# Retention and RWKV-7 mixer: a shorter chain from the keys to the decayed products, and head outputs summed in one PSUM bank

## The chip, the cores and the metric

The kernel runs on one core of a Trainium2 chip. The core has five engines with their own instruction queues: TensorE (matmuls, PE in the profile, with PEld for its weight loads), VectorE (DVE), ScalarE (ACT), GpSimd (POOL) and SyncE (SP), which only issues DMAs here. Matmul results go to PSUM, which has eight banks; everything else works in SBUF. The metric is the device time of one execution in microseconds (us); smaller is better.

## The reference

The program computes a decoder trunk of two layers for 1024 tokens of width 1024, in float32. Layer 0 is a mixer of two head groups that share one input projection: eight retention heads and eight RWKV-7 heads of 64 dimensions. Layer 1 is sliding-window attention. A SwiGLU network follows each. Only the mixer of layer 0 is changed. Of it, these are the lines that matter:

```python
decay = jnp.exp(-jnp.exp(w_log))
a = jax.nn.sigmoid(a0 + al @ a_up)
kkf = heads(kr * k_k)
kk = kkf / jnp.maximum(jnp.linalg.norm(kkf, axis=-1, keepdims=True), 1e-12)
kr = kr * (1.0 + (a - 1.0) * k_a)
# per token: state = state * w + (state @ a_t) b_t + v k, with a_t = -kk, b_t = kk * a
y = rwkv7_scan(r_h, heads(decay), k_h, v_h, -kk, kk * heads(a))
o = o_inner + o_cross          # retention: inside a chunk, and from the state before it
```

The decay of a token is exp(-c s), with c = exp(-0.5) and s the sigmoid of a projected value. Inside a chunk of 64 tokens the kernel needs the products of decays up to and including each token (the inclusive ones) and up to the token before it (the exclusive ones), and the reciprocals of the inclusive ones.

## The kernel before, in words

Channels lie on the 128 partitions and tokens in the free dimension. The sequence is worked in two halves of 512 tokens. A pair is two heads, one on partitions 0 to 63 and one on 64 to 127; there are four pairs of RWKV heads and four of retention heads for each half, so eight of each in all. A pair's tile is 128x512: eight chunks of 64 tokens for RWKV, four of 128 for retention.

`mixer0` sets up generators and lets the `Plan` class order them. Jobs are input projections (line 239 is the helper through which all mixer matmuls go; a job is 24 matmuls of 128x512 into a bank of the PSUM tag "f"). Chains are generators that yield after each step the events they need and a delay. The planner keeps an estimated time, advanced by each matmul. It runs the next step of a chain when its events and delay have passed and `room()` says that fewer than three PSUM tiles of the tag "m" were opened in the last 3 us of that estimate, and otherwise three matmuls of the current job. After the program is traced, the compiler's scheduler fixes each engine's order and gives out the tiles' memory: a tag has so many buffers, and a new tile of it has to wait until one is released. Each engine then works in its fixed order.

- `pair` (from line 655) is the chain of one RWKV pair. Step 1 (lines 666 to 676): scales the keys by the column kk, squares them (line 668), takes two tanh, turns one into the sigmoid s (673), scans it to its running sum in each chunk (cs, line 675), and subtracts s from that on GpSimd (676), which gives the running sum without the own token. Step 2 (680 to 702): sums of squares over a head by a matmul with a block matrix, their reciprocal root by Ln and Exp (682, 683), three exponentials (inclusive decays pw 685, their reciprocals 686, exclusive decays 687), the last inclusive decay of each chunk (PC, 689), the normalized keys (690), the products AR (692) and BK (693 to 696, copied by 697, other keys 701 and 702). Step 3 multiplies AR with BK on TensorE. Step 4 (729) multiplies r with pw on GpSimd into AR's other half. Later steps build masked products GG (754), their transposes and the values UV.
- `unit` (from line 813) takes two pairs of one half: it inverts triangular blocks on VectorE (836, 840), runs the recurrence over the eight chunks (938), and then forms the head outputs y (945 to 959): a sum within the chunk, from UV and GG, and one from the state before it, from GT and AR. Each sum has a PSUM bank; ScalarE copies one out (955), VectorE adds the other (956), ScalarE squares the result (958). Normalization and gate follow.
- `ret` is the chain of one retention pair; lines 1088 to 1099 form its outputs in the same way, with ScalarE's copy at 1096, VectorE's addition at 1097 and the square at 1099.

In these chains the short-lived 128x512 tiles have the tag "rt" with six buffers: kk, rn, s, ta, cs and pw of a pair, and y and q of a unit's two pairs. GpSimd also splits weights for the projections (331), after a cast on ScalarE (330).

## Time and profile before

| | us |
|---|---|
| median of three timed runs | 2411.41 |
| the three runs | 2411.33, 2411.41, 2417.50 |
| the profiled execution | 2407.97 |
| its span, first to last instruction | 2406.2 |

| engine | busy in the span, us | share |
|---|---|---|
| TensorE matmul | 2327.4 | 97% |
| TensorE weight loads | 1836.9 | 76% |
| VectorE | 1631.0 | 68% |
| ScalarE | 1036.0 | 43% |
| GpSimd | 1208.5 | 50% |

A row of a group of instructions in the profile reads: line, engine, operation, output tile <- input tiles, count, then least, median and greatest duration in ns, first and last start in us, and shape. A row of the timeline reads: start, duration, engine, line, operation, tiles, shape and count of like instructions in a row, and in brackets the idle time before it and what ended that. A row of waits reads: the waiting engine with its output tile and line, what it waited for, then the total in us, the number of waits and the longest. Busy time of TensorE has modelled ends, so a busy TensorE isn't one at its peak. The granted clock of TensorE is a share of full speed; its mean over the span is 0.988.

### The profile page before, as it was taken

To read this page: it belongs to the slowest core of one execution; us is meant where nothing else is said; L and a number is where in the kernel's file an instruction comes from. 1 tells how busy PE (TensorE), PEld (TensorE's weight loads), DVE (VectorE), ACT (ScalarE), POOL (GpSimd) and SP (SyncE) were. 2 spreads that over 40 slices of the span, in tenths; PEclk is the share of its full clock that TensorE was granted. 3 is DMA by queue.
4 is the path that set the end of the run, shared out by engine and by line. 5 is a ranking of instruction groups with operands and counts; after the bars stand their busy time and mean duration, and the time that the engine had idled before them with its cause. 6 is when DMAs were issued, how large, how long until landed. Compare 5 with 4: busy or idle time off the path is not lost. (4 is left out here: it accounts for less than half of the span.)

```text
span 2406.2 us, 35718 instructions
## 1 busy us (share of the span) xinstructions
PE 2327.4 (97%) x13098; PEld 1836.9 (76%) x13098; DVE 1631.0 (68%) x2478; ACT 1036.0 (43%) x1914; POOL 1208.5 (50%) x975
## 2 busy tenths in 40 slices
PE   8899999989999999999999999999999999999997
PEld 6676767777777888888778877677688788887785
DVE  5766765766557457887675459558628788888666
ACT  5353543223555433333333545456635233333336
POOL 6555332221443047776577632342231677777666
PEclk9999999999999999999999999999999999999999
DMA  7564543444345645553564322132236466646652
GB/s 250 197 214 171 165 155 123 143 119 124 122 171 166 213 155 207 215 204 135 198 249 148 127 75 64 53 134 67 94 123 216 158 215 217 215 182 248 242 201 108
DMA packets 167742, 395.93 MB, mean 165 GB/s; under 512 B 42896, under 2 KB 45584, under 8 KB 167568
## 3 DMA queue, kind: packets, MB, share of 16 engines
q1 hardware_dynamic: 164448, 388.15, 47.5%
q10 hardware_dynamic: 2832, 4.45, 0.5%
q8 instruction: 104, 1.70, 0.3%
q0 software_dynamic: 288, 1.05, 0.1%
q14 instruction: 70, 0.57, 0.1%
HBM read 271.29 MB, written 116.92 MB: 161 GB/s over the span
## 5 line engine op out<-in xcount | busy, mean ns | idle before, releaser
L331 POOL TENSOR_TENSOR w<-wr,w 128x512 fp32r<-128x512 f32 x196 | 266.3, 1365 | 444.3 <-ACT w L330 386.7
L239 PE MATMUL ps_f<-n,w 128*128 128x512 f32 x1440 | 384.4, 415 | 13.6 <-ACT w L330 5.9
L239 PEld LDWEIGHTS ps_f<-n,w 128*128 128x128 f32 x1440 | 268.4, 192 | 97.1 <-issue 22.0
L330 ACT CAST w<-wr 128x512 fp32r<-128x512 f32 x244 | 147.9, 612 | 180.1 <-PE ps_f L347 74.1
L331 POOL TENSOR_TENSOR w<-wq,w 128x512 fp32r<-128x512 f32 x92 | 130.0, 1424 | 32.6 <-ACT w L330 28.1
L345 PE MATMUL ps_f<-n,w 128*128 128x512 f32 x356 | 141.6, 398 | 2.4 <-ACT n L351 1.5
L346 PE MATMUL ps_f<-n,w 128*128 128x512 f32 x356 | 142.0, 399 | 0.0
L347 PE MATMUL ps_f<-n,w 128*128 128x512 f32 x356 | 140.5, 395 | 0.0
L1169 PE MATMUL ps_f<-n,w 128*128 128x512 f32 x322 | 127.1, 396 | 4.5 <-DVE h L1369 2.2
L1176 DVE TENSOR_TENSOR nq<-ps_m,u 128x512 f32<-128x512 f32 x88 | 58.8, 684 | 105.8 <-PE ps_m L1171 105.7
L1170 PE MATMUL ps_f<-n,w 128*128 128x512 f32 x322 | 126.3, 392 | 0.0
L1171 PE MATMUL ps_f<-n,w 128*128 128x512 f32 x322 | 125.6, 391 | 0.0
L353 POOL TENSOR_TENSOR n<-nq,n 128x512 fp32r<-128x512 f32 x64 | 107.0, 1684 | 10.7 <-ACT n L351 10.7
L1169 PE MATMUL ps_m<-n,w 128*128 128x512 f32 x282 | 110.5, 392 | 0.0
L1171 PE MATMUL ps_m<-n,w 128*128 128x512 f32 x282 | 109.9, 390 | 0.0
L1170 PE MATMUL ps_m<-n,w 128*128 128x512 f32 x282 | 109.7, 389 | 0.0
L331 POOL TENSOR_TENSOR wx<-wr,wx 128x512 fp32r<-128x512 f32 (+1 forms) x38 | 49.3, 1298 | 104.4 <-ACT wx L330 97.7
L1169 PE MATMUL ps_m<-cb,w 128*128 128x512 f32 x240 | 93.5, 389 | 0.9 <-DVE nq L1176 0.9
L1170 PE MATMUL ps_m<-cb,w 128*128 128x512 f32 x240 | 93.4, 389 | 0.0
L1171 PE MATMUL ps_m<-cb,w 128*128 128x512 f32 x240 | 93.4, 389 | 0.0
L1343 POOL TENSOR_TENSOR w<-wd,w 128x512 fp32r<-128x512 f32 (+1 forms) x53 | 76.5, 1455 | 33.3 <-ACT w L1342 33.3
L345 PEld LDWEIGHTS ps_f<-n,w 128*128 128x128 f32 x356 | 67.1, 189 | 20.1 <-issue 2.2
(525 smaller groups left out, 6496.8 us busy)
## 6 DMA issues: line engine op xcount, KB each, us to landing
hc<-n SPq DMA_DIRECT2D x74, 512.0 KB, 2.6
wsp<-w SPq DMA_DIRECT2D x54, 512.0 KB, 3.4
w<-wsp SPq DMA_DIRECT2D x54, 512.0 KB, 3.8
wq<-in_w_gate SPq DMA_DIRECT2D x44, 512.0 KB, 4.3
u<-u SPq DMA_DIRECT2D x88, 256.0 KB, 3.0
n<-hc SPq DMA_DIRECT2D x43, 512.0 KB, 5.4
wr<-in_w_in SPq DMA_DIRECT2D x34, 512.0 KB, 4.6
hid<-n SPq DMA_DIRECT2D x66, 256.0 KB, 2.0
```

Of the source, the lines that this page charges most:

```text
L239: self.nc.tensor.matmul(out, lhsT, rhs, **kw)
L330: nc.scalar.copy(hi[:, :n], raw[:, c])
L331: self.lo.tensor_tensor(out=lo[:, :n], in0=raw[:, c], in1=hi.bitcast(F32)[:, :n], op=ALU.subtract)
L345: nc.tensor.matmul(ps, hi, rh, start=k == 0, stop=False)
L346: nc.tensor.matmul(ps, hi, rl, start=False, stop=False)
L347: nc.tensor.matmul(ps, lo, rh, start=False, stop=k == n - 1)
L353: e.tensor_tensor(out=lo, in0=src, in1=hi.bitcast(F32), op=ALU.subtract)
L1169: mm(ps, hi, xh, start=first and k == 0, stop=False, skip_group_check=True)
L1170: mm(ps, hi, xl, start=False, stop=False, skip_group_check=True)
L1171: mm(ps, lo, xh, start=False, stop=last and k == len(w) - 1, skip_group_check=True)
L1176: add = lambda o, x, y: V.tensor_tensor(out=o, in0=x, in1=y, op=ALU.add)
L1343: nc.gpsimd.tensor_tensor(out=lo, in0=v, in1=hi.bitcast(F32), op=ALU.subtract)
```

## The change

In `pair`:

- the keys are no longer scaled into a tile of their own; the square takes the column as its scale, and the normalized keys come from one instruction that multiplies key, column and reciprocal root
- the subtraction and the third exponential go; the inclusive decays are written to a tile `pe` of eight rows of 66, from place 1 on, with a 1.0 filled in at place 0, and the exclusive decays are the same rows read from place 0. `pe` has one buffer, its own tag, and lives until line 729 has read it
- the factor -(1 + tanh)/2 is no longer a tile; (ta + 1) times the keys is one instruction, and the -0.5 goes into the one that makes BK
- the tag "rt" has five buffers instead of six

In `unit` and in `ret`: both sums are accumulated in one PSUM bank. Only the first matmul of each half of the partitions starts a group; it is kept in program order, and the rest is put behind it on TensorE. VectorE copies the bank out and ScalarE squares from it.

```diff
         k = self.pr[hf, p, "k"]
-        kk = self.t(mp, [P, HT], "rt", 6)
-        V.tensor_scalar(out=kk, in0=k, scalar1=self.col("kk", p), scalar2=None, op0=ALU.mult)
-        rn = self.t(mp, [P, HT], "rt", 6)
-        S.activation(rn, kk, AF.Square)
+        rn = self.t(mp, [P, HT], "rt", 5)
+        S.activation(rn, k, AF.Square, scale=self.col("kk", p))
...
         V.tensor_tensor_scan(cs, self.cst["smask"], s, 0.0, ALU.mult, ALU.add)
-        G.tensor_tensor(out=s, in0=cs, in1=s, op=ALU.subtract)
+        pe = self.t(mp, [P, NCH, 66], "pe", 1)
+        G.memset(pe[:, :, 0:1], 1.0)
         yield (), 8.5
...
-        pw = self.t(mp, [P, HT], "rt", 6)
-        S.activation(pw, cs, AF.Exp, scale=-CW)
+        pw = pe[:, :, 1:65]
+        S.activation(pw, c3(cs), AF.Exp, scale=-CW)
         S.activation(cs, cs, AF.Exp, scale=CW)
-        S.activation(s, s, AF.Exp, scale=-CW)
         PC = self.t(mp, [P, NCH], "PC", 4)
-        G.tensor_copy(PC, c3(pw)[:, :, 63])
-        V.tensor_tensor(out=kk, in0=kk, in1=rn, op=ALU.mult)
+        G.tensor_copy(PC, pe[:, :, 64])
+        V.scalar_tensor_tensor(out=rn, in0=k, scalar=self.col("kk", p), in1=rn, op0=ALU.mult, op1=ALU.mult)
         AR = self.t(mp, [P, NCH, P], "AR", 4)
-        V.tensor_tensor(out=AR[:, :, 0:64], in0=c3(kk), in1=c3(s), op=ALU.mult)
-        V.tensor_scalar(out=rn, in0=ta, scalar1=-0.5, scalar2=-0.5, op0=ALU.mult, op1=ALU.add)
-        V.tensor_tensor(out=rn, in0=rn, in1=kk, op=ALU.mult)
+        V.tensor_tensor(out=AR[:, :, 0:64], in0=c3(rn), in1=pe[:, :, 0:64], op=ALU.mult)
+        V.scalar_tensor_tensor(out=s, in0=ta, scalar=1.0, in1=rn, op0=ALU.add, op1=ALU.mult)
         BK = self.t(self.mz, [P, NCH, 3, 64], "BK", 2)
-        V.tensor_tensor(out=BK[:, :, 0, :], in0=c3(rn), in1=c3(cs), op=ALU.mult)
+        V.scalar_tensor_tensor(out=BK[:, :, 0, :], in0=c3(s), scalar=-0.5, in1=c3(cs), op0=ALU.mult, op1=ALU.mult)
...
-        G.tensor_tensor(out=AR[:, :, 64:128], in0=c3(r), in1=c3(pw), op=ALU.mult)
+        G.tensor_tensor(out=AR[:, :, 64:128], in0=c3(r), in1=pw, op=ALU.mult)
...
-            y1, y2 = self.pst("m", [P, NCH, 64]), self.pst("m", [P, NCH, 64])
-            for c in range(NCH):
-                for e, a in enumerate(half):
-                    self.mm(y1[a, c, :], UV[:, c, e, :], GG[:, c, e, 64:P], start=True, stop=True)
-            for c in range(NCH):
-                for a in half:
-                    self.mm(y2[a, c, :], GT[a, c, :], AR[a, c, 64:P], start=True, stop=True)
-            y = self.t(mp, [P, HT], "rt", 6)
-            S.copy(y, y1.rearrange("p c t -> p (c t)"))
-            V.tensor_tensor(out=y, in0=y2.rearrange("p c t -> p (c t)"), in1=y, op=ALU.add)
-            q = self.t(mp, [P, HT], "rt", 6)
-            S.activation(q, y, AF.Square)
+            ps = self.pst("m", [P, NCH, 64])
+            for e, a in enumerate(half):
+                i = self.mm(
+                    ps[a, 0, :], UV[:, 0, e, :], GG[:, 0, e, 64:P], start=True, stop=False, skip_group_check=True
+                )
+            self.keep(i)
+            kw = dict(start=False, skip_group_check=True)
+            with self.tc.issue_after(i.ins):
+                for c in range(1, NCH):
+                    for e, a in enumerate(half):
+                        self.mm(ps[a, c, :], UV[:, c, e, :], GG[:, c, e, 64:P], stop=False, **kw)
+                for c in range(NCH):
+                    for a in half:
+                        self.mm(ps[a, c, :], GT[a, c, :], AR[a, c, 64:P], stop=c == NCH - 1, **kw)
+            y = self.t(mp, [P, HT], "rt", 5)
+            V.tensor_copy(y, ps.rearrange("p c t -> p (c t)"))
+            q = self.t(mp, [P, HT], "rt", 5)
+            S.activation(q, ps.rearrange("p c t -> p (c t)"), AF.Square)
```

The block in `ret` changes in the same way, with one bank `ps` in place of `p1` and `p2`, and four chunks of 128. The helper `mm` now returns its instruction, which `keep` and `issue_after` need.

## The prediction

> **What bounds the kernel now.** I read the granted clock and span first (one core, clock 0.988, nothing disturbed), then busy time by stretch, then who TensorE waited for, then the timeline around its longest waits.

> ```profile
> span 2406.2 us, 35718 instructions
> ...
> 40.00:690.00 650.00, 616.75 (x5451) 471.89 (x5450) 420.64 (x844) 268.48 (x438) 260.52 (x285) 0.98 0.48 153
> 690.00:2406.00 1716.00, 1679.38 (x7535) 1342.62 (x7533) 1191.32 (x1612) 745.60 (x1443) 924.34 (x658) 0.99 0.48 167
> ```

> The columns after the length are busy time of PE, PEld, DVE, ACT and POOL, then clock, DMA share and GB/s. All eight pair steps and four unit steps that the change touches lie in 40 to 690 us. There TensorE is busy 616.75 of 650 us, VectorE 420.64, ScalarE 268.48, GpSimd 260.52. TensorE sets the end, so work taken from the other three is worth only what it takes out of TensorE's 33 us of idle time, and what clock comes back with it. This is who ended that idle time, longest first, from TensorE's waits in the first 690 us (total, times, longest):

> ```profile
> PE ps_m L239 <- DVE BK L696: 5.0, 2, 3.8
> PE ps_f L239 <- POOL w L331: 3.9, 5, 2.2
> ...
> PE ps_m L249 <- DVE GG L754: 3.2, 3, 2.2
> PE ps_m L239 <- DVE GG L754: 3.2, 3, 2.6
> PE ps_m L239 <- DVE UV L790: 2.8, 1, 2.8
> PE ps_m L239 <- DVE UV L901: 2.0, 1, 2.0
> PE ps_m L239 <- DVE GT L938: 2.0, 1, 2.0
> PE ps_c L239 <- DVE GT L938: 1.8, 1, 1.8
> ```

> VectorE is behind most of them. Some are the pair step itself (BK, line 696), some are other work queued behind a pair step's instructions on VectorE. The waits that pair-step instructions precede, and the clock around three of them (windows as above):

> ```profile
> 67.17 1.15 PE L239 MATMUL ps_m<-AR,BK 64*64 64x64 f32 x32 [1.26 <-DVE BK L696]
> ...
> 87.68 1.71 PE L249 MATMUL ps_m<-c_ident,BK 64*128 64x64 f32 x16 [2.23 <-DVE GG L754]
> ...
> 488.43 1.98 PE L239 MATMUL ps_m<-AR,BK 64*64 64x64 f32 x32 [3.75 <-DVE BK L696]
> ```

> ```profile
> 60.00:70.00 10.00, 8.74 (x65) 6.17 (x64) 9.93 (x12) 3.64 (x8) 8.41 (x9) 1.00 0.73 268
> ...
> 220.00:231.00 11.00, 9.05 (x79) 6.76 (x74) 7.89 (x11) 1.83 (x4) 4.64 (x5) 0.84 0.30 120
> ...
> 484.00:498.00 14.00, 10.25 (x101) 8.01 (x102) 10.86 (x14) 5.79 (x12) 7.59 (x8) 0.76 0.14 16
> ```

> Around the 1.26 us wait the granted clock stays 1.00. In 220 to 231 us it is 0.84, a loss of 11 x 0.16 = 1.8 us of full clock; in 484 to 498 us 0.76, a loss of 3.4 us. So a wait of about 2 us or more can cost nearly its own length again.

> **The change, part by part.** These are the prices:

> ```profile
> L666 DVE TENSOR_SCALAR rt<-rkk,pv x8: 468/492/1136, 48.7 to 488.2; 128x512 f32<-128x512 f32 x8
> L676 POOL TENSOR_TENSOR rt<-rt,rt x8: 1270/1499/1742, 53.4 to 493.1; 128x512 f32<-128x512 f32 x8
> L689 POOL COPY PC<-rt x8: 184/194/658, 55.2 to 494.7; 128x8 f32<-128x8 f32 x8
> L687 ACT ACTIVATE rt<-rt x8: 613/616/633, 55.7 to 495.4; 128x512 f32<-128x512 f32 x8
> L690 DVE TENSOR_TENSOR rt<-rt,rt x8: 691/692/693, 60.8 to 504.0; 128x512 f32<-128x512 f32 x8
> L693 DVE TENSOR_SCALAR rt<-rt x8: 412/418/1506, 63.2 to 505.3; 128x512 f32<-128x512 f32 x8
> ...
> L973 DVE SCALAR_TENSOR_TENSOR rt<-rt,pv,rt x8: 750/752/1492, 245.1 to 697.3; 128x512 f32<-128x512 f32 x8
> ...
> L1104 ACT ACTIVATE r<-r,c_eps x8: 709/724/726, 138.0 to 649.2; 128x512 f32<-128x512 f32 x8
> ...
> L1578 DVE COPY pT<-ps_m x32: 672/682/692, 1419.3 to 1737.1; 128x512 f32<-128x512 f32 x32
> L1576 ACT COPY pT<-ps_m x28: 560/579/593, 1429.2 to 1736.7; 128x512 f32<-128x512 f32 x28
> ```

> *Pair step, engine time.* VectorE loses lines 666 and 693 (0.49 + 0.42 us), and one product becomes a three-operand form with a column scalar (0.752 in place of 0.692): 0.85 us less a pair, 6.8 us over eight. ScalarE loses line 687 (0.62) and its square gains a column scale; the nearest row with a column operand is line 1104 (0.724 against 0.616): 0.51 less, 4.1 us over eight. GpSimd loses line 676 (1.50) and gains a fill of 128x8, nearest line 689 (0.19): 1.3 less, 10.4 us over eight. None of that is on the path by itself: TensorE's products cover it. The path changes in four places.

> (a) At 67.17. Without line 676 the in-place exponential of line 686 no longer waits for GpSimd:

> ```profile
>   ACT rt L686: 2.9, 4
> ```

> (four waits for line 676, 0.7 us each); line 687 no longer stands ahead of the logarithm in ScalarE's order (0.62); line 693 no longer stands ahead of BK (0.42). The sum is 1.7 us, more than the 1.26 us wait, so the wait goes: -1.26.

> (b) At 87.68 the masked product of line 754 stands on VectorE behind the other pair's line 693: -0.42 of 2.23.

> (c) At 223.94, by the timelines of VectorE, TensorE and GpSimd:

> ```profile
> 218.50 0.68 DVE L692 TENSOR_TENSOR AR<-rt,rt 128x512 f32<-128x512 f32 x1
> 219.10 1.51 DVE L693 TENSOR_SCALAR rt<-rt 128x512 f32<-128x512 f32 x1
> 220.64 1.64 DVE L694 TENSOR_TENSOR rt<-rt,rt 128x512 f32<-128x512 f32 x1
> 222.21 1.48 DVE L698 TENSOR_SCALAR rt<-rt,hk 128x512 f32<-128x512 f32 x1
> 223.61 0.46 DVE L938 SCALAR_TENSOR_TENSOR GT<-ps_c,PC,XA 128x64 f32<-128x64 f32 x2
> ```

> ```profile
> 219.18 0.45 PE L239 MATMUL ps_c<-GT,XA 64*64 64x64 f32 x8
> ...
> 223.94 0.33 PE L239 MATMUL ps_m<-AR,GT 64*64 64x64 f32 x4 [1.95 <-DVE GT L938]
> ```

> ```profile
> 218.60 1.73 POOL L331 TENSOR_TENSOR w<-wr,w 128x512 fp32r<-128x512 f32 x1 [1.91 <-ACT w L330]
> 220.29 3.12 POOL L543 TENSOR_TENSOR nq<-nq,nq 128x512 f32<-128x512 f32 x2
> ```

> Line 938 has its products by 219.63 and stands behind three pair-step instructions, each stretched to about 1.5 us and ending just after a GpSimd instruction ends. With line 693 gone, line 694 takes its place and all behind it moves up one: -1.51, and the remaining 0.44 us is shorter than the wait at 67 us that cost no clock, so the 1.8 us come back too: -3.3. The other bound is line 693's undisturbed 0.42.

> [...]

> (d) At 488.43: line 693 stood ahead of BK once: -0.42 of 3.75, the clock still drops.

> *Head outputs.* The number and shape of matmuls stay. ScalarE's copy out of the first bank goes (16 times about 0.58: 9.3 us). VectorE's add becomes a copy out of PSUM (0.68). The square reads PSUM instead of SBUF, 0.58 by line 1576. The two readers of the one bank must take turns, as the copies of lines 900 and 901 do (line 900's wait for the other):

> ```profile
>   DVE UV L901: 7.4, 10
> ```

> So copy then square is as long as add then square was: 0. The wait that it adds holds ScalarE's queue for at most 0.68 us; behind it stand casts of weights (line 330), and their low halves on GpSimd (line 331) are what TensorE waited for 3.9 us in five waits. One such wait lost or won: within 0.7 us either way. Two banks fewer per unit step and one fewer per retention step: no row of TensorE's waits names lines 955, 956, 1096 or 1097, so I take 0.

> *Buffers.* A pair held six of six tiles of the tag and now holds four of five; a unit's four y and q tiles want room among them, so the shortage shrinks. The single tile of decays must be free when the next pair fills its column. The closest case is the first two pairs, last reader (line 729) against the next pair's first step:

> ```profile
> 55.38 1.29 POOL L729 TENSOR_TENSOR AR<-rr,rt 128x512 f32<-128x512 f32 x1
> ...
> 68.84 0.49 DVE L666 TENSOR_SCALAR rt<-rkk,pv 128x512 f32<-128x512 f32 x1
> ```

> It is free 12.2 us ahead: 0. If the order moved the next pair ahead by that much, weight splits on GpSimd would queue behind the fill.

> *Strided decays.* Three instructions a pair read or write rows of 66 instead of 64. I take 0, since AR and BK are in blocks already; the dear bound is one more 0.69 us at (c) and (d): +1.4.

> **Sum**: -1.26 - 0.42 - 3.3 - 0.42 = -5.4 us. The profiled execution took 2407.97 us (span 2406.2 plus 1.8 outside it), so its like would take 2402.6. The median of the three timed runs is 2411.41, 3.4 above it; on that scale the forecast is **2406.0 us**.

> **The rivals.** *Spread gain.* The stalls that I left alone (UV at lines 790 and 901, 2.8 and 2.0; the rest of BK, 3.3, with its 3.4 us of clock; GG in line 239, 2.6) lie behind a VectorE with 6.8 us less to do and less GpSimd beside it. If all went, with 1.8 us of clock for each but BK, it would be -(2.8 + 2.0 + 2.6 + 3 x 1.8 + 6.7) = -19.5 more, 2386; half of it is -15 in all, 2396. For it: VectorE ends most waits. Against: the waits at lines 790 and 754 (239) come from other chains' instructions, which stay.

> *Hidden anyway.* The four waits shrink, but the products that filled TensorE elsewhere are then missing elsewhere, and the waits reappear: 2411, within 2. For it: TensorE is 95% busy in the stage. Against: a lost clock window is a net loss.

> *Slower.* The planner counts PSUM banks: fewer than three in use in its 3 us lets the next chain step out ahead of projection products. A unit's output step took four and takes two, a retention step two and now one. At these twelve places dependent steps then come closer together with fewer products to cover them. Price of one new stall: a wait like that on line 790, 2.8, plus 1.8 of clock, 4.6. Two leave the sum at +3.8; from three on (+8.4) it is slower than can be told from no change: 2420. For it: waits of that kind exist already with four banks. Against: other chains' steps mostly have room then, and TensorE's queue holds products of all chains.

> *It does not do what it says.* If the compiler's order puts BK no earlier, (a), (b) and (d) fall away and -3.3 is left: 2408.

> [...]

> **How the numbers follow.** Forecast (-2 to -9, with "does not do what it says" inside): 0.40, a quarter of it beyond -7.2. Spread gain 0.23, all beyond -7.2. Hidden 0.21. Slower 0.16, of which 0.13 beyond +7.2. What a measurement of this kernel can tell is about 0.3%, 7.2 us. So faster 0.33, same 0.54, slower 0.13. The range of the forecast alone is 2402 to 2410; 8 in 10 takes the spread gain to three quarters and the first three new stalls: 2392 to 2418, the two unknown prices (0.7 and 1.4) inside.

> **What would show it.** Right: no wait on BK near 67 us, line 938 near 222 us with TensorE waiting under half a us and clock near 1.00 there; TensorE's busy time in the stage the same, its idle 3 to 4 us less; ScalarE about 13, GpSimd about 10 and VectorE about 7 us less busy. Wrong: new TensorE waits just behind unit or retention output steps; waits of GpSimd's fill on line 729's heir; an after with the same idle but other places; or a stage whose order differs so much that none of the four places can be found again.

## The result, and the profile after

The kernel after takes 2392.15 us (median of 6 runs, 2386.86 to 2394.37), the kernel before, on the same chip, 2412.66 us (6 runs, 2411.33 to 2419.89). The ratio is 0.9913, 95% interval 0.9898 to 0.9929: 20.5 us faster, where 5.4 us were forecast. The page of the kernel after, whose profiled execution took 2394.0 us:

```profile
span 2392.2 us, 35667 instructions
...
PE 2318.9 (97%) x13098; PEld 1828.7 (76%) x13098; DVE 1626.3 (68%) x2462; ACT 1025.5 (43%) x1890; POOL 1193.1 (50%) x975
```

To see where the time went I cut both profiles at the same product, behind the same 5,683 matmuls, when all pair, unit and retention steps are done. Busy time by stretch, columns as in the prediction, first the kernel before, then the kernel after:

```profile
0.00:720.50 720.50, 677.00 (x5683) 516.25 (x5684) 458.79 (x891) 312.69 (x503) 298.98 (x327) 0.98 0.50 163
```

```profile
0.00:702.75 702.75, 668.35 (x5683) 509.11 (x5684) 452.47 (x875) 301.31 (x479) 283.30 (x327) 0.99 0.52 167
```

The point is reached 17.75 us earlier. TensorE's idle time falls from 43.5 to 34.4 us (length less busy time), 9.1 us. Its busy time falls by 8.65 us for the same matmuls; most of that is clock, since the stretches at half clock go from nine of 3.41 us to five, which is worth 6.8 us. VectorE is 6.3 us less busy (6.8 forecast), ScalarE 11.4 (13.4), GpSimd 15.7 (10.4). Behind that point the program is the same but for a few neighbouring instructions that change places, and the kernel after takes 3.75 us longer there (TensorE is idle 38.9 us, before 35.3), so that the two profiled executions are 14.0 us apart. The 20.5 us are of medians; in these two profiles the stage up to the cut shows 17.75.

What TensorE waited for in the first 690 us of the kernel after (total, times, longest):

```profile
...
PE ps_f L239 <- DVE n L463: 3.4, 3, 1.9
PE ps_m L250 <- DVE GG L752: 2.5, 3, 1.0
PE ps_m L239 <- ACT rt L970: 2.3, 1, 2.3
...
PE ps_c L239 <- DVE GT L936: 2.1, 1, 2.1
PE ps_m L239 <- DVE AR L924: 2.0, 2, 1.3
PE ps_m L239 <- DVE XA L910: 1.8, 1, 1.8
PE ps_f L239 <- POOL w L332: 1.5, 2, 1.3
PE ps_m L239 <- DVE GG L752: 1.4, 2, 1.0
PE ps_m L239 <- DVE BK L694: 1.3, 1, 1.3
PE ps_m L239 <- DVE UV L899: 1.2, 1, 1.2
...
PE ps_m L239 <- DVE GT L936: 0.7, 1, 0.7
```

Beside the rows of before: BK 5.0 to 1.3, low halves of weights on GpSimd 3.9 to 1.5, GG 6.4 to 3.9 in both rows together, UV of the pair (line 790) 2.8 to nothing, UV of the unit 2.0 to 1.2, GT 2.0 to 0.7. Against it stand longer waits on ScalarE's normalization (line 970), AR and XA. No single wait holds the gain: it lies in a good half of the rows.

The kernel before had two more waits close together, which the forecast left alone:

```profile
428.85 1.66 PE L239 MATMUL ps_m<-UV,GG 64*64 64x64 f32 x32 [2.76 <-DVE UV L790]
...
438.04 1.48 PE L249 MATMUL ps_m<-c_ident,BK 64*128 64x64 f32 x16 [0.77 <-DVE GG L754]
```

The forecast's places (b), (c) and (d) in TensorE's timeline of the kernel after, and the clock in stretches around (c), around what had been 428.85 us, and around (d):

```profile
83.22 1.31 PE L250 MATMUL ps_m<-c_ident,BK 64*128 64x64 f32 x16 [0.94 <-DVE GG L752]
...
215.98 0.33 PE L239 MATMUL ps_m<-AR,GT 64*64 64x64 f32 x4 [0.69 <-DVE GT L936]
...
470.04 1.15 PE L239 MATMUL ps_m<-AR,BK 64*64 64x64 f32 x32 [1.30 <-DVE BK L694]
```

```profile
212.00:223.00 11.00, 10.31 (x114) 7.85 (x111) 7.12 (x13) 1.72 (x3) 5.96 (x7) 1.00 0.24 84
405.00:425.00 20.00, 20.00 (x206) 16.31 (x206) 13.72 (x37) 4.71 (x9) 2.18 (x3) 1.00 0.48 139
465.00:479.00 14.00, 12.70 (x197) 9.47 (x198) 11.84 (x16) 7.03 (x16) 6.46 (x9) 1.00 0.18 53
```

The waits are 0.94, 0.69 and 1.30 us, and the clock stays up around (c) and (d) and in the middle stretch, where TensorE has no idle time at all. Added up, the waits at (b), (c) and (d) fall by 1.29, 1.26 and 2.45 us and the two at 428.85 and 438.04 by 3.53: 8.5 of the 9.1 us, while the other waits nearly cancel out. Six of the nine stretches at half clock in the kernel before begin at or just behind these waits, none of the five in the kernel after.

### The profile page after: what moved, and what is told of

It reads as the page before. It is cut to its first block, busy times and chain, and to the rows that moved or that the text cites. A ratio compares the mean times of both kernels' runs of the same rounds, so it can differ in the third digit from the quotient of the medians.

```text
span 2392.2 us, 35667 instructions
## 1 busy us (share of the span) xinstructions
PE 2318.9 (97%) x13098; PEld 1828.7 (76%) x13098; DVE 1626.3 (68%) x2462; ACT 1025.5 (43%) x1890; POOL 1193.1 (50%) x975
## 5 line engine op out<-in xcount | busy, mean ns | idle before, releaser
L239 PE MATMUL ps_f<-n,w 128*128 128x512 f32 x1440 | 383.5, 414 | 12.0 <-ACT w L331 6.4
L239 PEld LDWEIGHTS ps_f<-n,w 128*128 128x128 f32 x1440 | 268.3, 192 | 93.3 <-issue 21.9
L331 ACT CAST w<-wr 128x512 fp32r<-128x512 f32 x244 | 147.9, 612 | 188.8 <-PE ps_f L348 76.9
```

The costliest lines, as they stand in the source:

```text
L239: i = self.nc.tensor.matmul(out, lhsT, rhs, **kw)
L331: nc.scalar.copy(hi[:, :n], raw[:, c])
```

## The experiments

The kernel before ran beside each of them on the same chip. The ratio and its interval come from the single executions, so it need not be the ratio of the two medians.

| kernel | median us (range) | before | ratio [95% interval] |
|---|---|---|---|
| keys' part alone | 2399.61 (2399.22 to 2407.16) | 2411.13 | 0.9952 [0.9939, 0.9966] |
| sums' part alone | 2403.17 (2396.03 to 2411.48) | 2411.13 | 0.9967 [0.9955, 0.9979] |
| after, planner told of old banks | 2392.65 (2387.21 to 2394.03) | 2411.13 | 0.9915 [0.9902, 0.9928] |
| before, planner told of new banks | 2409.90 (2404.04 to 2416.37) | 2411.13 | 0.9993 [0.9982, 1.0004] |
| late tile | 2406.75 (2401.57 to 2412.51) | 2412.61 | 0.9972 [0.9960, 0.9985] |
| retention's sum alone | 2412.69 (2407.55 to 2416.06) | 2412.61 | 1.0000 [0.9988, 1.0012] |
| products alone, 6 tiles | 2411.62 (2407.20 to 2417.31) | 2412.61 | 0.9996 [0.9983, 1.0009] |
| products alone, 5 tiles | 2402.58 (2400.94 to 2404.15) | 2412.61 | 0.9958 [0.9942, 0.9974] |
| before without swap | 2404.87 (2402.05 to 2409.46) | 2412.31 | 0.9980 [0.9968, 0.9992] |
| after without swap | 2390.69 (2388.04 to 2397.07) | 2412.31 | 0.9919 [0.9902, 0.9936] |
| before, second step 10.5 | 2422.97 (2417.81 to 2429.07) | 2412.31 | 1.0051 [1.0034, 1.0068] |
| after, second step 10.5 | 2403.64 (2400.89 to 2412.62) | 2412.31 | 0.9970 [0.9958, 0.9982] |
| before, third step 14 | 2424.40 (2422.40 to 2429.84) | 2413.09 | 1.0056 [1.0035, 1.0076] |
| after, third step 14 | 2395.19 (2392.67 to 2396.03) | 2413.09 | 0.9928 [0.9912, 0.9945] |
| before, second step 6.5 | 2417.99 (2411.57 to 2423.66) | 2411.59 | 1.0029 [1.0015, 1.0043] |
| after, second step 6.5 | 2398.24 (2392.79 to 2403.64) | 2411.59 | 0.9950 [0.9931, 0.9968] |
| after, all pair work back | 2399.92 (2394.70 to 2404.23) | 2413.09 | 0.9950 [0.9930, 0.9969] |
| after, GpSimd's and ScalarE's back | 2398.32 (2395.08 to 2407.28) | 2413.09 | 0.9948 [0.9931, 0.9964] |

**Which part gains.** The first two kernels hold the diff's pair step alone (tag rt at 5, the decays' tile in) and its two output steps alone (tag rt at 6). The third takes the retention's output step alone. Their edits are those parts of the diff, shown with the change above.

> Only the change in the pair chain (and five rt buffers with the tile of decays); head outputs as before. Theory A (the gain is VectorE's, ScalarE's and GpSimd's shorter chain in front of TensorE's inputs): nearly all of the 20 us, 2391 to 2397. Theory B (the gain comes from the one bank for both sums): 2408 to 2412, nothing. Theory C (the gain is the planner's order, which follows the count of banks): 2408 to 2412.

> Only the accumulation of both sums in one bank, in the unit and retention chains, with six rt buffers; the pair chain as before. Theory A: 2409 to 2413, nothing. Theory B: 2391 to 2397. Theory C: 2391 to 2400, since the planner counts fewer banks here too.

> Before, with the sum in one bank in the retention step alone (eight steps); the unit's output step keeps two banks, tag rt keeps 6. Theory tiles: 2411, since the retention's tiles are of another tag and have room. Theory bank: about 2407, half of the 8 us that the sums alone gained, as half of the copies and eight of the twelve places are here. Theory work: 2407 too.

Keys -11.5 us, sums -8.0, together -19.5 beside -20.5 for both: neither theory that gave all to one part holds, and both times lie outside what any of the three theories gave. The retention's sum is worth nothing (2412.69 against 2412.61), which leaves the 8 us to the unit's output step. That the two parts add up so well is in part chance, since both contain one and the same stall, as is seen below. The two parts at place (c), keys first, then sums:

```profile
220.19 0.33 PE L239 MATMUL ps_m<-AR,GT 64*64 64x64 f32 x4 [0.69 <-DVE GT L936]
```

```profile
221.76 0.37 PE L239 MATMUL ps_m<-AR,GT 64*64 64x64 f32 x4 [1.96 <-DVE GT L939]
```

With the sums alone the wait is that of before; with the keys alone it is the 0.69 us of after. So (c) is the keys' work, as forecast.

**The planner's count of banks.** The kernel after with one more bank counted at each sum, as many as before, and the kernel before with one less counted at each pair of banks:

```diff
+            self.plan.banks.append(self.plan.now + 3.0)
```

```diff
+            self.plan.banks.pop()
```

> The changed kernel, but the planner is told of as many PSUM banks at the head outputs as before (an entry in its list, no bank is taken), so its order is that of the old count. Theories A and B: 2390 to 2396, as the changed kernel. Theory C: 2405 to 2412, the gain gone.

> The kernel before, with two banks for the two sums, but the planner is told of one. Theories A and B: 2409 to 2413. Theory C: 2391 to 2400, the gain without the change of work.

Both stay where they were, and in the traces the order of every engine's instructions is the same with and without the count, but for two neighbouring matmuls of the kernel after. The rival "slower" has no ground here: the planner's count decides nothing in this stage. The two runs serve as second executions of the same order: TensorE's idle time up to the cut is 42.4 us in the one of before and 33.9 in the one of after, close to the 43.5 and 34.4 above.

**Same work in another order.** In the kernel before, the first bank is copied out as soon as it is full; the tile for the sum is thus taken early. "Late tile" swaps the two banks' roles, with no instruction more or less:

```diff
-            S.copy(y, y1.rearrange("p c t -> p (c t)"))
-            V.tensor_tensor(out=y, in0=y2.rearrange("p c t -> p (c t)"), in1=y, op=ALU.add)
+            S.copy(y, y2.rearrange("p c t -> p (c t)"))
+            V.tensor_tensor(out=y, in0=y1.rearrange("p c t -> p (c t)"), in1=y, op=ALU.add)
```

> Before, with one edit in the unit's output step: ScalarE copies the second bank of the two out first and VectorE adds the first bank to it. Both banks, all instructions and their number stay; only the tile that holds the sum is taken later, when the second bank is full. Theory tiles (sums in one bank gain because the sum's tile of tag rt is taken later, so that the next pair's decays find a tile): about 2403, as with the sums alone, and the two waits near 428 and 438 us go. Theory bank (the gain is the freed PSUM bank) and theory work (the gain is ScalarE's copy that is gone): 2411, those waits stay.

"Products alone" fuses the keys' products on VectorE and leaves the subtraction and the third exponential, once with 6 tiles of tag rt and once with 5:

```diff
-        kk = self.t(mp, [P, HT], "rt", 6)
-        V.tensor_scalar(out=kk, in0=k, scalar1=self.col("kk", p), scalar2=None, op0=ALU.mult)
-        S.activation(rn, kk, AF.Square)
+        S.activation(rn, k, AF.Square, scale=self.col("kk", p))
...
-        V.tensor_scalar(out=rn, in0=ta, scalar1=-0.5, scalar2=-0.5, op0=ALU.mult, op1=ALU.add)
-        V.tensor_tensor(out=rn, in0=rn, in1=kk, op=ALU.mult)
+        V.scalar_tensor_tensor(out=s, in0=ta, scalar=1.0, in1=rn, op0=ALU.add, op1=ALU.mult)
```

> Before, with the keys' products in fewer VectorE steps (line 666 gone, lines 690 to 696 as in the kernel after); GpSimd's subtraction and the third exponential stay, and so do two banks. A pair then uses five tiles of tag rt of six: one is spare. Theory tiles: the spare tile is what counts, so about 2400 as with the keys' part alone. Theory work (VectorE's and GpSimd's shorter queues, by share of engine time): about 2405 to 2407, since GpSimd's 10.4 us stay.

> The same with tag rt at 5 tiles, so that none is spare. Theory tiles: the gain is lost again, 2410 to 2415. Theory work: as with six tiles, 2405 to 2407.

The late tile gains 5.9 us with the same work, between the two times expected for it. The products alone gain nothing with a spare tile and 10 us without one: the reverse of what the theory on tiles had. That theory falls as I put it, and the theory on work, 2405 to 2407, misses both too. What the runs show is that the number of tiles and the moment at which one is taken change the compiled order, and that the order alone is worth 6 to 9 us. One place where it acts can be read. VectorE before TensorE's wait of 2.76 us at 428.85, in the kernel before:

```profile
416.67 0.69 DVE L777 TENSOR_REDUCE vm<-ps_m 128x8 f32<-128x512 f32 x1
423.29 0.69 DVE L997 TENSOR_TENSOR r<-r,c_sin 128x512 f32<-128x512 f32 x1 [5.93 <-DMA r<-r]
...
425.95 0.42 DVE L781 TENSOR_TENSOR UV<-ps_m,vm 64x256 f32<-64x256 f32 x1
...
428.28 0.43 DVE L790 TENSOR_TENSOR UV<-ps_m,vm 64x256 f32<-64x256 f32 x1
```

Line 997 belongs to the retention and waits 5.93 us for its swap of halves by DMA; the pair's UV instructions stand behind it, with their transposes done. The same stretch of the kernel after, where the swapped product is line 1001:

```profile
406.52 0.42 DVE L779 TENSOR_TENSOR UV<-ps_m,vm 64x256 f32<-64x256 f32 x1 [0.32 <-POOL vm L776]
...
409.01 0.43 DVE L788 TENSOR_TENSOR UV<-ps_m,vm 64x256 f32<-64x256 f32 x1 [0.32 <-POOL vm L776]
...
413.96 0.69 DVE L1001 TENSOR_TENSOR r<-r,c_sin 128x512 f32<-128x512 f32 x1 [2.72 <-DMA r<-r]
```

Here it stands behind UV, waits 2.72 us, and TensorE does not wait. With the products alone it is the same contrast, first 6 tiles (VectorE, then TensorE), where the wait stands ahead of UV and TensorE then waits 2.23 us for line 788, then 5 tiles, where it comes before the transposes and TensorE does not wait:

```profile
420.60 0.69 DVE L995 TENSOR_TENSOR r<-r,c_sin 128x512 f32<-128x512 f32 x1 [5.51 <-DMA r<-r]
```

```profile
426.57 2.04 PE L239 MATMUL ps_m<-UV,GG 64*64 64x64 f32 x32 [2.23 <-DVE UV L788]
```

```profile
411.50 0.69 DVE L995 TENSOR_TENSOR r<-r,c_sin 128x512 f32<-128x512 f32 x1 [3.19 <-DMA r<-r]
```

The other kernels that keep the planner's numbers and the swap divide in the same way. With the second execution of before and with the retention's sum alone, the swap's wait in this place is 6.02 and 6.45 us and TensorE waits 2.83 and 3.27 us for the pair's UV; with the keys alone, the sums alone and the late tile it is 1.67, 2.68 and 1.62 us and TensorE does not wait for it. All kernels of the first group run at 2409.9 us and more, those of the second at 2406.8 and less. So the 11.5 us of the keys, the 8.0 of the sums, the 10 of the products with 5 tiles and the 5.9 of the late tile all contain this one stall, which can be won only once.

**The swap taken away.** If that DMA wait makes the stalls near 429 and 438 us, leaving the swap out should take them from the kernel before:

```diff
-                for a in range(4):
-                    b = a ^ 1
-                    nc.sync.dma_start(sw[32 * a : 32 * a + 32], raw[32 * b : 32 * b + 32])
-                G.tensor_tensor(out=raw, in0=raw, in1=cos, op=ALU.mult)
-                V.tensor_tensor(out=sw, in0=sw, in1=sin, op=ALU.mult)
+                V.tensor_tensor(out=sw, in0=raw, in1=sin, op=ALU.mult)
+                G.tensor_tensor(out=raw, in0=raw, in1=cos, op=ALU.mult)
```

> Before, without the retention's swap of halves: the four DMAs are left out and line 997 multiplies the unswapped tile, so queries and keys are not rotated as they should be; the instructions of VectorE and GpSimd stay. In the profile before, line 997 waits 22 us in all for that swap, once 5.9 us with the pair's UV instructions behind it, just ahead of TensorE's wait of 2.8 at 428.85. Theory swap (that wait, which holds VectorE's queue, makes the stalls near 429 and 438 us and their lost clock, 7 us, and the change wins by moving line 997 behind the UV): 2404, those stalls gone. Otherwise: 2409 to 2412, the stall on UV there still.

> After, with the same left out. Theory swap: little to gain, 2389 to 2392, so that the lead over the kernel before with the same left out shrinks from 20 to about 13. Otherwise: the lead stays at about 20.

The kernel before gains 7.4 us, the kernel after 1.5 (2390.69 against 2392.15, measured on different occasions, so hardly more than nothing), and the lead shrinks from 20.5 to 14.2 us, as the theory on the swap had it. In TensorE's timeline of the kernel before without the swap the product on UV has no wait:

```profile
429.35 1.15 PE L239 MATMUL ps_m<-UV,GG 64*64 64x64 f32 x32
```

So about 6 us of the 20.5 come from the swap's DMA waits, and the stall at 428.85 is the one that is seen to go. Taking the swap away also reorders the program and takes the swap's other waits, so the 6 us are not all proved to be this one place.

**The lead in other orders.** If a third of the lead is where things happen to land, is the rest too? Two of the planner's numbers were changed in both kernels, one of them in two ways, which adds no work and changes the order:

```diff
-        yield (), 8.5
+        yield (), 10.5
```

(6.5 in another pair of kernels; in the third pair the next step's 12.0 became 14.0.)

> Before, with one number of the planner changed: the pair's second step comes 10.5 us after its first in place of 8.5. No instruction is added or removed; only the order changes. Theory work (the 20 us come from the shorter queues of VectorE, GpSimd and ScalarE): 2411, within 3, and the kernel after with the same number keeps its lead of 18 to 22. Theory order (most of it is where dependent steps land in the queues): moves by 5 or more either way, 2403 to 2419.

> After, with the same number 10.5 in place of 8.5. Theory work: 18 to 22 below the kernel before with the same number. Theory order: the lead is another one, under 15 or over 25.

> Before, with another number of the planner changed: the pair's third step comes 14 us after its second in place of 12. A third order for the same instructions. Nothing says which way its time goes: 2400 to 2425.

> After, with the same number 14. Under two orders the lead was 20.3 and 19.3 us. If the lead comes from what the change does wherever the steps land, it is 15 to 25 again; if two agreeing leads were chance, it is outside that.

> Before, with the pair's second step 6.5 us after its first in place of 8.5. A fourth order. If steps that come later only cost (10.5 and 14 cost 11 and 11 us), earlier steps may win: 2400 to 2412. If BK and the logarithm are then not ready and the queues behind them wait, 2415 or more.

> After, with the same number 6.5. Three leads were 20, 19 and 29 us. If the lead comes from what the change does in any order: 15 to 30 below the kernel before with the same number, which may beat both kernels (2385 to 2395).

The kernel before loses 10.7, 11.3 and 6.4 us by these orders, so order moves it by more than my whole forecast, and with 10.5 by more than either theory gave (2403 to 2419). The leads of after over before are 20.5, 19.3, 29.2 and 19.8 us, in the order of the table. The third was outside the 15 to 25 that I expected. TensorE up to the same product as above, as length less busy time, and busy time:

| second, third step | idle before, after (us) | busy before, after (us) |
|---|---|---|
| 8.5, 12 | 43.5, 34.4 | 677.0, 668.4 |
| 10.5, 12 | 55.0, 40.8 | 681.0, 675.3 |
| 8.5, 14 | 50.7, 36.8 | 682.1, 671.9 |
| 6.5, 12 | 47.3, 36.3 | 680.7, 673.1 |

In each order the change takes 9 to 14 us of idle time and 6 to 10 us of busy time. The waits that go are not the same ones. With second step 10.5 or 6.5 the kernel before has no wait of more than 0.7 us on the pair's UV, and the lead is there all the same. The lead of about 20 us is therefore no stroke of luck of one order; which waits carry it is.

**The work put back.** The kernel after with the pair's removed work as work without use; in the first kernel all four lines, in the second the two of GpSimd and ScalarE alone:

```diff
+        V.tensor_scalar(out=k, in0=k, scalar1=1.0, scalar2=None, op0=ALU.mult)
+        G.tensor_tensor(out=s, in0=cs, in1=s, op=ALU.subtract)
+        S.activation(s, s, AF.Exp, scale=-CW)
+        V.tensor_scalar(out=ta, in0=ta, scalar1=1.0, scalar2=0.0, op0=ALU.mult, op1=ALU.add)
```

> After, with the pair's removed work put back as work without use, in the same places: GpSimd's subtraction and the third exponential write a tile that nobody reads before it is overwritten, and VectorE multiplies the key tile and the tanh tile by 1 in place. The decays stay in their own tile and the sums in one bank. Theory work (the keys' part gains by work and length of the chain): its 12 us are lost, 2402 to 2406. Theory tiles (it gains because the decays have a tile of their own and the six slots are no longer short): 2390 to 2395.

> After, with GpSimd's subtraction and the third exponential alone put back as work without use. Theory work, shared by engine time: about half of the 12 us lost, 2396 to 2400; if GpSimd's 1.5 us beside VectorE is the whole of it, 2402 to 2406. Theory tiles: 2390 to 2395.

They are 13.2 and 14.8 us under the kernel before, so 7.3 and 5.7 of the 20.5 us are lost; by the ratios both are some 12 us under it. The first lies 2 us under what the theory on work gave, the second within its 2396 to 2400, and both lie above what the theory on tiles gave. The two are not clearly apart, so nearly all that the work is seen to be worth is GpSimd's and ScalarE's. One link can be read. GpSimd and then TensorE in the kernel with the subtraction back:

```profile
73.08 1.29 POOL L675 TENSOR_TENSOR rt<-rt,rt 128x512 f32<-128x512 f32 x1
...
75.61 3.76 POOL L332 TENSOR_TENSOR w<-wr,w 128x512 fp32r<-128x512 f32 x3
```

```profile
76.94 1.21 PE L239 MATMUL ps_f<-n,w 128*128 128x512 f32 x4 [1.14 <-POOL w L332]
```

The subtraction stands ahead of the low halves of the weights, and TensorE waits 1.14 us for them. The kernel before has the same at 78.72 us:

```profile
78.72 1.21 PE L239 MATMUL ps_f<-n,w 128*128 128x512 f32 x4 [1.11 <-POOL w L331]
```

In the kernel after there is no wait there. At (c) and (d) the kernel with the subtraction back has 1.13 and 1.30 us, beside 0.69 and 1.30 of after: (d) does not need the subtraction gone.

None of these kernels beats the kernel after by a margin; the numbers that it has for the planner are the best of the four orders tried, for before as for after.

## Why the prediction was right or wrong

The direction was right, and so were three of the four places. The size was not: 20.5 us for 5.4. The result is at the very edge of my range of 2392 to 2418 and in the rival *spread gain* (2386 to 2396), which I had given 0.23. That rival came nearest in its mechanism too: of the waits that it names, the pair's UV went, and BK (5.0 to 1.3), line 239's GG (3.2 to 1.4) and the unit's UV (2.0 to 1.2) shrank.

*(a), at 67.17.* The wait is gone. But the second execution of before's order has none there either, so this 1.26 us is not to be counted for the change:

```profile
66.79 1.15 PE L239 MATMUL ps_m<-AR,BK 64*64 64x64 f32 x32
```

*(b), -0.42 forecast.* 2.23 became 0.94, -1.3 us. The clock, which fell at 88 us in the kernel before, stayed up (0.89 from 86 to 101 us there, 1.00 from 83 to 98 here).

*(c), -1.51 and 1.8 of clock.* 1.95 became 0.69, -1.26 us, with the keys' part alone too, and the clock is 1.00. The first two of the instructions still ahead are as stretched as their like before (1.51 and 1.64 us there), in VectorE's timeline of the kernel after:

```profile
211.83 1.75 DVE L692 SCALAR_TENSOR_TENSOR rt<-rt,rt 128x512 f32<-128x512 f32 x1
213.61 1.66 DVE L694 SCALAR_TENSOR_TENSOR BK<-rt,rt 128x512 f32<-128x512 f32 x1
215.20 0.53 DVE L696 TENSOR_SCALAR rt<-rt,hk 128x512 f32<-128x512 f32 x1
215.65 0.46 DVE L936 SCALAR_TENSOR_TENSOR GT<-ps_c,PC,XA 128x64 f32<-128x64 f32 x2
```

One instruction fewer stands ahead of GT, and the next ones take 1.75 and 1.66 us in its place, as the prediction had it. That the price was to be 1.51 and not the undisturbed 0.42 us was my estimate, and no run shows by itself what makes the stretch. What the traces show is GpSimd beside it: in the kernel after two of its instructions, of 1.71 and 1.73 us, begin at 211.32 and 212.99, and line 696, which begins when GpSimd is idle, takes 0.53 us, where its like in the kernel before, line 698, took 1.48 beside GpSimd's line 543. The clock part of the forecast, 1.8 us, was of one execution (last section).

*(d), -0.42 forecast.* 3.75 became 1.30, -2.45 us, and the clock of 0.76 became 1.00, another 3.4 us. VectorE from the key product to BK, before and after:

```profile
481.82 0.69 DVE L690 TENSOR_TENSOR rt<-rt,rt 128x512 f32<-128x512 f32 x1 [2.64 <-ACT rt L683]
...
483.63 0.42 DVE L693 TENSOR_SCALAR rt<-rt 128x512 f32<-128x512 f32 x1
484.09 1.41 DVE L694 TENSOR_TENSOR rt<-rt,rt 128x512 f32<-128x512 f32 x1
485.42 0.53 DVE L698 TENSOR_SCALAR rt<-rt,hk 128x512 f32<-128x512 f32 x1
485.88 0.74 DVE L626 SCALAR_TENSOR_TENSOR rkk<-rkk,pv,z 128x512 f32<-128x512 f32 x1
486.54 1.74 DVE L696 TENSOR_TENSOR BK<-rt,rt 128x512 f32<-128x512 f32 x1
```

```profile
465.90 0.75 DVE L689 SCALAR_TENSOR_TENSOR rt<-rkk,pv,rt 128x512 f32<-128x512 f32 x1 [2.64 <-ACT rt L683]
...
467.76 0.68 DVE L692 SCALAR_TENSOR_TENSOR rt<-rt,rt 128x512 f32<-128x512 f32 x1
468.48 1.41 DVE L694 SCALAR_TENSOR_TENSOR BK<-rt,rt 128x512 f32<-128x512 f32 x1
469.82 0.53 DVE L696 TENSOR_SCALAR rt<-rt,hk 128x512 f32<-128x512 f32 x1
470.27 0.74 DVE L627 SCALAR_TENSOR_TENSOR rkk<-rkk,pv,z 128x512 f32<-128x512 f32 x1
```

From the key product's start to BK's end it was 6.46 us and is 3.99. Line 693 is 0.42 of the 2.47. The rest is that BK now stands ahead of two others (lines 698 and 626 of before, 0.46 and 0.66 by their starts), that the product before it is no longer stretched (1.41 to 0.68), and that BK itself is less so (1.74 to 1.41). Here is the step that failed: I took an instruction out of a list and let everything else keep its place. The fused products are enough for the new place: in the traces of the products alone with 6 tiles, of the keys alone and of the kernels with the subtraction and with all work put back, BK stands ahead of both instructions at (d) too, and TensorE waits 0.56, 1.30, 1.30 and 1.34 us (with 5 tiles it stands ahead of line 698's heir alone); with the sums alone and with the late tile, whose products are not fused, it stands behind them, and the waits are 2.61 and 3.06. That the compiler moves BK because it is ready a step earlier is my reading; no run shows its reasons. At (a), too, a 1.50 us instruction (line 698) stood ahead of BK, and the bare duration of the removed line was never the price.

*Head outputs, 0 forecast.* Wrong: -8.0 us with the sums alone. That copy and square take the same time as add and square did was right (0.68 and 0.60 us, before 0.68 and 0.63); that nothing else follows was not. The runs put it in the unit's output step, and 5.9 us can be had there by taking the tile later with all work kept; both lose the stall at 428.85. The retention's half is 0, as forecast.

*Buffers, 0 forecast.* Wrong: one tile more or fewer of tag rt, with the same instructions, is worth 9 us (2411.62 against 2402.58). I had priced only a wait for a free tile; the count acts through the order, which differs between these two kernels on every engine.

*Spread gain, the argument against it.* "The waits at lines 790 and 754 (239) come from other chains' instructions, which stay." They stay, but what stands ahead of them does not: 2.8 us on line 790 went to 0 with a DMA-bound instruction of the retention moved behind it, and line 754's 3.2 us went to 1.4.

*Engine work covered by TensorE's products.* "None of that is on the path by itself" was too strong. With the tiles and the one bank kept, putting the work back costs some 7 us.

*Hidden anyway* fell, and so did *slower*, with its ground. What stays open: how the 20 us divide over work and order. The runs give some 7 us for the pair's work and some 6 us for the swap, each with other orders mixed in, and the unit's 8 us was seen in one order only.

## What to carry to other kernels

Where many chains share in-order queues under a compiler that reorders, price a removed instruction by the length from the chain's first step to the product that TensorE waits for, and look at every other instruction that may change sides, not at the one line. Before believing a gain or a loss of half a percent, run both kernels under a few other orders of the same work: here order alone was worth 6 to 11 us, and only the lead over four orders showed what belonged to the change. An instruction that waits for a DMA in a shared queue is worth finding first: read what stands behind it.

## What the runs showed of the hardware

The clock. Over the profiles of all 20 kernels I counted TensorE's waits of 1 us and more between 40 and 700 us that did not begin at a lower clock, and how many had the granted clock fall to half from within the wait until 3.4 us behind it:

```
wait of TensorE     waits   clock fell
1.0 to 1.5 us        101       13
1.5 to 2.0 us         54       32
2.0 to 2.5 us         46       31
2.5 us and more       43       43
```

Each fall in this stage lasts 3.41 us or a multiple of it, up to four times, at a granted clock of 0.50, and so costs half of its length: in the kernel before five last 3.41 us and two 6.83. Behind waits between 1.5 and 2.5 us the clock fell 63 times in 100, and not always alike behind the same wait in the same order. The kernel before with the new count of banks has the wait at (c) with the same 1.95 us, and its clock stays up (0.84 in the kernel before), TensorE's timeline and then the stretch around it:

```profile
222.71 0.33 PE L239 MATMUL ps_m<-AR,GT 64*64 64x64 f32 x4 [1.95 <-DVE GT L938]
```

```profile
219.00:230.00 11.00, 9.05 (x91) 6.68 (x87) 7.89 (x13) 1.73 (x3) 5.10 (x5) 1.00 0.33 124
```

So my 1.8 us of clock at (c) were the price of one execution, not of the wait.

```
idle in the piece      pieces   clock fell
under 1.0 us           1808        4
1.0 to 1.7 us           150       27
1.7 to 2.0 us            33       27
2.0 us and more          64       64
```

In these profiles, then, a fall followed 4 of the 1808 pieces with under 1.0 us of idle time, 27 of the 150 pieces with 1.0 to 1.7 us and 91 of the 97 with 1.7 us and more. These are counts; what lies behind them no run shows. At (c) the whole wait, 221.99 to 223.94 us, lies in the piece from 221.43 to 224.84 of the kernel before. In its second execution a piece ends at 221.85, in the middle of the same wait from 220.76 to 222.71, and neither side holds more than 1.1 us of it.

Executions of one order differ, and the longer ones had the lower clock: the kernel before ran from 2404.82 to 2419.62 us in 29 executions on one chip, on average 2417.2 us in the four with a mean clock of 0.985 and 2408.0 us in the four with 0.989.
